# Feed-forward in: two groups of weight columns taken product by product on both sides of the change of token halves

## The chip, the cores and the metric

The kernel runs on one core of one Trainium2 chip. The metric is the device time of one execution in microseconds (us). Of the core's engines, PE (TensorE) multiplies matrices, PEld is its weight load, DVE (VectorE) and ACT (ScalarE) do elementwise work, POOL (GpSimd) does elementwise work too, and SP (SyncE) issues the DMAs here, all from one queue in program order. Every engine works through its own instructions strictly in order.

## The reference, cut to what matters

One layer of a decoder with 2048 tokens and a width of 1024. The attention and gated-linear-attention part ahead of the change is untouched; what the change touches is the first product of the feed-forward block, `nm @ w_ff1`, and what is done with its result:

```python
def rmsnorm(x, g):
    y = x * lax.rsqrt(jnp.mean(x * x, axis=-1, keepdims=True) + EPS)
    return y * g
...
    h = h + jnp.einsum('bsm,md->bsd', mixed, w_out[l])
    nm = rmsnorm(h, mlp_norm_g[l])
    a = jnp.square(jax.nn.relu(jnp.einsum('bsd,df->bsf', nm, w_ff1[l])))   # (2048,1024) x (1024,4096)
    h = h + jnp.einsum('bsf,fd->bsd', a, w_ff2[l])
return rmsnorm(h, final_norm_g)
```

## The kernel before, in words

Every float32 product is made of three products of split numbers: each operand is cut into a high part (a copy in the reduced type, made by ACT) and a low part (operand minus high part, made by DVE), and `mm3` (lines 131 to 134) multiplies high by high, low by high and high by low.

The feed-forward product is done with a scheme of Strassen's kind: seven block products, numbered j = 1 to 7 and taken in the order 1, 2, 5, 6, 3, 4, 7, in place of eight. A *group* g is 256 columns of `w_ff1` against one half (1024) of the tokens. There are NP = 16 groups for each half, so groups 0 to 15 use the first token half and 16 to 31 the second: 32 groups of 7 products, 224 in all, listed in `jobs1`. One product is four calls of `mm3`, 12 matmuls of 128x128 by 128x512, into one PSUM bank. The stationary operand is a weight block (`w1comb`, four buffers in turn), the moving operand a token block `TF[j]` (the tiles `hb...`: for each j a high and a low tile of 2048 columns, 14 tiles that stay in SBUF for a whole token half).

Products 6 and 7 go on adding into the bank in which product 1 stands (`U1`), and product 3 into that of product 5 (`W1B`); so the copy of the bank that is taken after product 1, 5 or 6 has to be done before the later product of the same group starts.

The order of the work is written by hand: inside `tc.manual_schedule(...)` the instructions of all five engines stand as the loop issues them. For each place `at` in `jobs1` the loop calls `slot1(at)`, then steps of the sums over finished groups, then `product1(at)`. `slot1(at)` issues:

- `hi1(at + 3)` on ACT and `lo1(at + 2)` on DVE: the high and low part of the weight block of a coming product (lines 1442 and 1447);
- `evict1(at - 1)`: what is taken out of the bank of the product before: a copy by ACT for j = 1, 6, 5, 4 (lines 1490 to 1494), additions by DVE for j = 2, 3 (one each) and 7 (two; lines 1496 to 1501). The copy of j = 1 and 6 goes to a tile `X`, which is `xt`;
- `squares1(at)`: Relu and Square on ACT (lines 1508, 1509), in pairs, four pairs a group;
- `sum1`, four a group on DVE (line 1454): sums of the raw weight blocks, made in place in `w1raw`, on which some of the coming `hi1` wait;
- `load_w1`, a 1 MB load of the raw weight columns of group g + 2.

When a pair of groups (14 products) is done, `token_sums` makes 28 sums of 128x256 tiles of it (line 1547) during the 14 products that follow, and stores them to `actD` in DRAM, each store eight steps behind its sum in SP's queue. The table `SUMS` gives 11 of them to POOL and 17 to DVE; where `all_pool[0]` is set, POOL makes all 28. The tiles (`acc1`, and the second halves of `xt` and of `gM`) are overwritten by the evictions of the next pair but one.

The change of halves lies at product 112 of 224, the first of group 16. The 14 tiles of `TF` have to be refilled with the second half: for each j a load of 1 MB from `hTD` into a raw tile `rb`, and then, in two parts of 1024 columns each, a high part by ACT (line 549) and a low part by DVE (line 550); 14 such parts in all. In the kernel before, group 15 is the last to use the old tiles and group 16 the first to use the new ones, so a tile `TF[j]` is read by product j of group 15 and again, refilled, seven products later by product j of group 16. The 14 parts are issued at products 106 to 116 (`parts_at`), and three `rb` tiles take the loads in turn.

Of the kernel before, what the change touches and what calls it, by code (L numbers as in the profile page):

```python
# [106 lines left out]
def emit(tc, a, stop=99):  # L107
    nc = tc.nc
    V, A, G, T, SP = nc.vector, nc.scalar, nc.gpsimd, nc.tensor, nc.sync
# [39 lines left out]
    xt = const.tile([128, 1024], F32, name="xt")  # L149
# [61 lines left out]
    hTD = dram.tile([2, 7, 128, 4, 512], F32, name="hTD")  # L211
# [14 lines left out]
    order = (1, 2, 6, 5, 7, 4, 3)  # L226
# [11 lines left out]
    TF = {j: [slot(f"tb{j}", FR) for _ in range(2)] for j in order[:3]}  # L238
# [7 lines left out]
    CX, last, c11, c22, c12, c21 = [t[:, GP * q:GP * q + GP] for t in acc for q in range(2)]  # L246
# [62 lines left out]
    def bank():  # L309
        btags.append(btags.pop(0))  # L310
        return ps(btags[-1])
# [147 lines left out]
    for g in range(NG):  # L459
# [3 lines left out]
        for x, j in enumerate(order):  # L463
            at, b = 7 * g + x, B + L * x
            h, l = (b - 5, b - 3) if L == 2 or (early and x == 0) else (b - 7, b - 4)
            if L == 4 and x == 2:
                h, l = b - 6, b - 3
            if g in (7, 8) or g == 9 and x < 2:
                h, l = b - 3, b - 2
# [51 lines left out]
    rb, oh = bp[:33, :8], view(bp[:33, 8:], (3, 384))  # L521
# [26 lines left out]
    def split(hi, lo, src):  # L548
        A.activation(hi, src, AF.Copy)
        V.tensor_tensor(lo, src, hi.bitcast(F32), op=OP.subtract)  # L550
# [81 lines left out]
    for n in range(7):  # L632
        t = base[7] + 6 + 23 * n // 4
# [99 lines left out]
    with tc.manual_schedule(engines={X.engine for X in (T, V, A, G, SP)}):  # L733
# [78 lines left out]
        for t in range(3, 8):  # L812
            n = t + 1
# [23 lines left out]
        for t in range(12, base[NG] + 10):  # L837
# [436 lines left out]
    for pr in range(4):  # L1274
# [3 lines left out]
        for hh, br in seq:  # L1278
            b = Branch()
            b.h, b.br = 2 * pr + hh, br  # L1280
            m = 4 if br == 2 else 2
            first = len(units)
# [3 lines left out]
            if br == 2 and first:  # L1286
# [61 lines left out]
    gM, gF = gs[:, :D], gs[:, D:2 * D]  # L1348
# [3 lines left out]
    rb, TF, TB = [slot("rb")], {}, {}  # L1352
# [19 lines left out]
    turns = [0]  # L1372
    order = (1, 2, 5, 6, 3, 4, 7)

    def reload(j, half, t=None):

        if t is None:
            t = rb[turns[0] % len(rb)]
            turns[0] += 1
        SP.dma_start(t[:, :2048], hTD[half, j - 1].rearrange("p c s -> p (c s)"))  # L1380

        def rest():
            if j not in TF:
# [29 lines left out]

    w1 = a["w_ff1"].rearrange("o (c p) n -> p (o c) n", p=128)
    NP = FF // 256
    jobs1 = [(g, j) for g in range(2 * NP) for j in order]
    raw1, combs1, acc1 = [], [], []

    def load_w1(g):
        if g < 2 * NP:  # L1420
            if len(raw1) < 2:
                raw1.append(view(slot("w1raw"), (CH, 256)))
            g0 = g % NP * 256
            SP.dma_start(raw1[g % 2], w1[:, :, g0:g0 + 256])

    def blocks1(g):
        r = raw1[g % 2]
        return [r[:, 4 * k:4 * k + 4, n * 128:n * 128 + 128] for n in range(2) for k in range(2)]

    def comb1(at):  # L1430
# [8 lines left out]
    def hi1(at):  # L1439
        if at < len(jobs1):  # L1440
            c, v = comb1(at)
            A.activation(c[:, 0], v, AF.Copy)  # L1442

    def lo1(at):
        if at < len(jobs1):
            c, v = comb1(at)
            V.tensor_tensor(c[:, 1], v, c[:, 0].bitcast(F32), op=OP.subtract)  # L1447

    def sum1(g, n):

        if g < 2 * NP:
            a11, a12, a21, a22 = blocks1(g)
            to, x, y = ((a21, a21, a22), (a11, a21, a11), (a12, a12, a11), (a21, a22, a11))[n]
            V.tensor_tensor(to, x, y, op=OP.subtract if n else OP.add)
# [25 lines left out]
    def blocks_of(g):  # L1480
        return [acc1[g % 4][:, 512 * n:512 * n + 512] for n in range(4)]

    def evict1(at):

        if not 0 <= at < len(jobs1):
            return
        g, j = jobs1[at]
        X, (c11, c12, c21, c22) = xt[:, :512], blocks_of(g)
        if j in (1, 6):
            A.activation(X, U1[g % 2], AF.Copy)  # L1490
        elif j == 5:
            A.activation(c22, W1B[g % 2], AF.Copy)
        elif j == 4:
            A.activation(c21, Y1[g % 2], AF.Copy)
        elif j == 2:
            V.tensor_tensor(c11, Y1[g % 2], X, op=OP.add)
        elif j == 3:
            V.tensor_tensor(c12, W1B[g % 2], X, op=OP.add)
        else:
            V.tensor_tensor(c21, U1[g % 2], c21, op=OP.add)  # L1500
            V.tensor_tensor(c22, U1[g % 2], c22, op=OP.add)
# [8 lines left out]

    def slot1(at):

        g, i = divmod(at, 7)
        hi1(at + 3)
        lo1(at + 2)
        evict1(at - 1)
        squares1(at)
        for k, gg, n in ((5, g + 1, 0), (6, g + 1, 1), (0, g, 2), (1, g, 3)):
            if i == k:
                sum1(gg, n)  # L1520
        if i == 5:
            load_w1(g + 2)

    def act_tiles(g):

# [4 lines left out]
    all_pool = [False]  # L1530
# [219 lines left out]
    for q, at in enumerate(first_of):  # L1750
# [5 lines left out]
        for u in range(4):  # L1756
            n = at + ((-11, -8, -4, -2) if q else (-10, -8, -5, -2))[u]
# [21 lines left out]
            product1(at)  # L1779

    with tc.manual_schedule(engines={X.engine for X in (T, V, A, G, SP)}):
        first, parts_at = 7 * (NP - 1), {}
        for n in range(14):
            parts_at.setdefault(first + 1 + n * 4 // 5, []).append(n // 2)
        halves, begun, half_done = {}, {}, set()
        ts = iter(())
        for at in range(7, len(jobs1)):
            if at == first - 3:
                rb.append(slot("rb"))
                turns[0] = 0  # L1790
                halves.update({n: reload(order[n], 1) for n in range(3)})
            slot1(at)
            all_pool[0] = first < at < first + 13 or at >= len(jobs1) - 6
            if at % 14 == 0:
                for _ in ts:
                    pass
                if at:
                    ts = token_sums(at // 7 - 1)
            for _ in range(SUMS_AT.get(at % 14, 0) if at > 13 else 0):
                next(ts)  # L1800
            product1(at)
            for n in [n for n in begun if n < 4 and begun[n] < at and n + 3 not in halves]:
                halves[n + 3] = reload(order[n + 3], 1)
            for n in parts_at.get(at, ()):
                next(halves[n])
                if n in half_done:
                    begun[n] = at
                half_done.add(n)
            for n in range(2):
                step(2 * (at - len(jobs1)) + n)  # L1810

        for _ in ts:
            pass
        ts = token_sums(2 * NP - 1)
        P, left = {}, None
        for ph in range(2 * NR):
            if PRODUCTS[ph // 2][1]:
                P[ph % 2] = [bank() for _ in range(2)]
            p = P[ph % 2]
            for k in range(8):  # L1820
# [74 lines left out]
```

## Time and profile before

| | |
|---|---|
| median of 3 runs | 2257.23 us (2255.97 to 2259.64) |
| the profiled execution, its own time | 2256.31 us |
| its span, first to last instruction | 2254.5 us |
| mean granted TensorE clock | 0.998 |
| PE busy | 2229.1 us, 99% of the span |
| PEld, DVE, ACT, POOL busy | 85%, 71%, 52%, 36% of the span |

Times inside the trace are us from the start of the span. The first feed-forward product runs from 1057 to 1675 us. A row of the timeline gives the start of an instruction, its length, its engine, its line, operation and tiles, how many it merges, and in brackets the idle time of the engine just before it with what ended it. A row of the waits gives who waited for whom, the total in us, how many times, and the longest. Neighbouring instructions overlap a little, so what one costs its engine is the distance from its start to the next one's start.

### The profile page before, as it was taken

How to read it: one execution, taken by the hardware profiler on the slowest of the kernel's cores; microseconds unless marked ns; L12 is line 12 of the kernel's file. 1: busy time of each engine (PE TensorE's matmuls, PEld its weight loads, DVE VectorE, ACT ScalarE, POOL GpSimd, SP SyncE). 2: the span in 40 equal slices, each digit the busy share in tenths (PEclk: the TensorE clock that was granted, in tenths of full speed). 3: DMA queues.
4: the chain of work that ended last, by engine and by line, in shares of the span. 5: the costliest groups of instructions: out<-in, count | busy, mean ns of one | idle time of the engine just before them, and what ended most of it. 6: DMA issues, size and time to landing. Idle time of an engine off the chain costs nothing.

```text
span 2254.5 us, 34335 instructions
## 1 busy us (share of the span) xinstructions
PE 2229.1 (99%) x12324; PEld 1925.5 (85%) x12324; DVE 1605.4 (71%) x2757; ACT 1164.0 (52%) x2088; POOL 812.5 (36%) x802
## 2 busy tenths in 40 slices
PE   9999999999999999999999999999999999999998
PEld 7978998899999998888888887888888888888886
DVE  6866767746766784446677779777776878758897
ACT  6554446435777782234555557555563333323544
POOL 2111000005378766300122235232345645232665
PEclk9999999999999999999999999999999999999999
DMA  7256444757657864777344457444488653454563
GB/s 207 87 179 194 131 137 153 256 177 238 217 194 240 280 208 150 225 243 263 115 150 145 150 187 226 143 146 148 137 273 306 202 169 130 142 168 149 174 219 112
DMA packets 308267, 415.23 MB, mean 184 GB/s; under 512 B 19509, under 2 KB 236126, under 8 KB 302464
## 3 DMA queue, kind: packets, MB, share of 16 engines
q1 hardware_dynamic: 307950, 412.77, 57.1%
q8 instruction: 97, 1.59, 0.3%
q14 instruction: 74, 0.61, 0.1%
q10 hardware_dynamic: 146, 0.27, 0.0%
HBM read 268.48 MB, written 149.20 MB: 185 GB/s over the span
## 4 chain that ended last, share of the span: by engine, by line
PE 91%; DVE 4%; issue 2%; DMA 1%; ACT 1%; POOL 0%; SPq 0%; POOLq 0%; ACTq 0%; DVEq 0%
PE ps_a L132 11%; PE ps_a L133 11%; PE ps_a L134 11%; PE ps_c L132 9%; PE ps_c L134 8%; PE ps_c L133 8%; PE ps_a L1005 5%; PE ps_d L133 4%; PE ps_d L132 4%; PE ps_d L134 4%; PE ps_d L986 3%; PE ps_c L966 2%; PE ps_c L964 2%; PE ps_o L132 2%; PE ps_o L134 2%; PE ps_o L133 2%
## 5 line engine op out<-in xcount | busy, mean ns | idle before, releaser
L1442 ACT ACTIVATE w1comb<-w1raw 128x512 fp32r<-128x512 f32 x224 | 141.4, 633 | 243.3 <-PE ps_a L134 81.8
L1624 ACT ACTIVATE cs<-rs 128x1024 fp32r<-128x1024 f32 x104 | 109.7, 1055 | 218.7 <-PE ps_c L134 127.8
L1447 DVE TENSOR_TENSOR w1comb<-w1raw,w1comb 128x512 fp32r<-128x512 f32 x224 | 175.8, 786 | 27.5 <-ACT w1comb L1442 27.5
L977 ACT ACTIVATE pe<-pe,O 128x256 f32<-128x256 f32 (+1 forms) x384 | 156.2, 454 | 62.2 <-DVE O L976 57.6
L1005 PE MATMUL ps_a<-v,pt 128*128 128x65 f32 x1200 | 179.0, 252 | 0.0
L1005 PEld LDWEIGHTS ps_a<-v,pt 128*128 128x128 f32 x1200 | 173.4, 193 | 0.9
L986 PE MATMUL ps_d<-ident,pe 128*128 128x128 f32 x600 | 158.1, 278 | 0.0
L976 DVE CUSTOM_DVE_ANT_0 pe<-ps_c,nb 128x256 f32<-128x256 f32 (+1 forms) x384 | 126.7, 361 | 41.5 <-PE ps_d L986 16.8
L132 PE MATMUL ps_a<-hb,w1comb 128*128 128x512 f32 x384 | 149.7, 390 | 0.0
L133 PE MATMUL ps_a<-hb,w1comb 128*128 128x512 f32 x384 | 149.5, 389 | 0.0
L134 PE MATMUL ps_a<-hb,w1comb 128*128 128x512 f32 x384 | 149.4, 389 | 0.0
L1666 DVE TENSOR_TENSOR ct<-rt,ct 128x1024 fp32r<-128x1024 f32 x68 | 129.8, 1909 | 18.8 <-ACT ct L1662 18.8
L133 PE MATMUL ps_c<-ct,cs 128*128 128x512 f32 x360 | 140.1, 389 | 0.0
L132 PE MATMUL ps_c<-ct,cs 128*128 128x512 f32 x360 | 140.1, 389 | 0.0
L134 PE MATMUL ps_c<-ct,cs 128*128 128x512 f32 x360 | 140.1, 389 | 0.0
L163 POOL TENSOR_TENSOR stats<-stats,mhalf 128x1 f32<-128x1 f32 (+1 forms) x64 | 50.0, 783 | 242.6 <-DVE stats L162 242.5
L918 POOL CAST qp<-qs 128x512 fp32r<-128x512 f32 x64 | 66.6, 1126 | 180.2 <-DMA srD<-xp 164.1
L1547 POOL TENSOR_TENSOR acc<-acc 128x256 f32<-128x256 f32 x75 | 69.1, 931 | 160.9 <-DVE acc L1547 148.6
L1631 DVE SCALAR_TENSOR_TENSOR cs<-rs,cs 128x1024 fp32r<-128x1024 f32 (+1 forms) x56 | 100.0, 1793 | 29.6 <-ACT cs L1624 29.3
L293 ACT ACTIVATE wcomb<-wraw 128x512 fp32r<-128x512 f32 (+2 forms) x119 | 89.1, 756 | 60.2 <-DVE wraw L305 25.2
L1547 POOL TENSOR_TENSOR xt<-acc,acc 128x256 f32<-128x256 f32 x32 | 28.1, 878 | 226.7 <-ACT acc L1509 210.3
L986 PEld LDWEIGHTS ps_d<-ident,pe 128*128 128x128 f32 x600 | 108.0, 185 | 0.3
(434 smaller groups left out, 7319.4 us busy)
## 6 DMA issues: line engine op xcount, KB each, us to landing
rs<-actD SPq DMA_DIRECT2D x103, 512.0 KB, 3.7
actD<-acc SPq DMA_DIRECT2D x288, 128.0 KB, 2.9
w1raw<-w_ff SPq DMA_DIRECT2D x32, 1024.0 KB, 6.5
rt<-w_ff SPq DMA_DIRECT2D x24, 1024.0 KB, 7.2
k<-kD SPq DMA_DIRECT2D x16, 1024.0 KB, 8.5
rb<-hTD SPq DMA_DIRECT2D x13, 1024.0 KB, 7.6
wraw<-w_in SPq DMA_DIRECT2D x12, 1024.0 KB, 5.3
cmb<-boD SPq DMA_DIRECT2D x16, 528.0 KB, 6.2
```

The costliest lines, as they stand in the source:

```text
L132: T.matmul(out, sh, mh, start=first, stop=False, skip_group_check=more)
L133: T.matmul(out, sl, mh, start=False, stop=False, skip_group_check=more)
L134: T.matmul(out, sh, ml, start=False, stop=last, skip_group_check=more)
L976: V.tensor_tensor_reduce(p, s, bias, scale=1.0, scalar=BIG, op0=OP.add, op1=OP.min, accum_out=nm)
L977: A.activation(p, p, AF.Exp, bias=nm, scale=-1.0)
L986: T.transpose(pb[:, i * 128:i * 128 + 128], src, ident)
L1005: T.matmul(self.b.opsum[:, n % 4], self.pt[:, i * 128:i * 128 + 128], self.b.v[:, blk, cols], start=first, stop=last)
L1442: A.activation(c[:, 0], v, AF.Copy)
L1447: V.tensor_tensor(c[:, 1], v, c[:, 0].bitcast(F32), op=OP.subtract)
L1624: A.activation(v[:, 0], x, AF.Copy, scale=float(PRODUCTS[ph // 2][2]))
L1631: V.scalar_tensor_tensor(v[:, 1], x, -1.0, v[:, 0].bitcast(F32), op0=OP.mult, op1=OP.subtract)
L1666: V.tensor_tensor(v[:, 1], x, v[:, 0].bitcast(F32), op=OP.subtract)
```

## The change

Four things are altered together.

1. `jobs1`, the order of the products. Groups 14 and 15 (the last two of the first half) and groups 16 and 17 (the first two of the second) are taken product by product: j = 1 of group 14, j = 1 of 15, j = 2 of 14, j = 2 of 15 and so on. All other groups stand as they did. A tile `TF[j]` is now read last by one of two neighbouring products and is needed again, refilled, from 12 products after them.
2. The refill: the 14 parts are spread over products 100 to 122 (`first` is 98), one part in a place, the high part at place `at` and the low part at the head of place `at + 1`. Their loads are 512 KB each, into the two halves of one `rb` tile, and the load of part m + 2 is issued behind the low part of m.
3. The weight sums stand one place earlier (in all groups), and there are four `w1raw` buffers in place of two. `X` is `xt` for even groups and `gM` for odd ones.
4. `all_pool` is set for places 100 to 124, where it was 106 to 117.

```diff
-    jobs1 = [(g, j) for g in range(2 * NP) for j in order]
+    jobs1 = []
+    for g in range(0, 2 * NP, 2):
+        if g in (NP - 2, NP):
+            jobs1.extend((g + k, j) for j in order for k in range(2))
+        else:
+            jobs1.extend((g + k, j) for k in range(2) for j in order)
+    at_of = {job: at for at, job in enumerate(jobs1)}
+    sums_at, loads_at = {}, {}
+    for g in range(2 * NP):
+        for n, j, dt in ((0, 5, 5), (1, 6, 5), (2, 3, 5), (3, 7, 6)):
+            if g or n > 1:
+                sums_at.setdefault(max(0, at_of[g, j] - dt), []).append((g, n))
+        loads_at[at_of[g, 1] - 9] = g
...
-            SP.dma_start(raw1[g % 2], w1[:, :, g0:g0 + 256])
+            SP.dma_start(raw1[g % 4], w1[:, :, g0:g0 + 256])
...
-        X, (c11, c12, c21, c22) = xt[:, :512], blocks_of(g)
+        X, (c11, c12, c21, c22) = (xt, gM)[g % 2][:, :512], blocks_of(g)
...
-        for k, gg, n in ((5, g + 1, 0), (6, g + 1, 1), (0, g, 2), (1, g, 3)):
-            if i == k:
-                sum1(gg, n)
-        if i == 5:
-            load_w1(g + 2)
+        for g, n in sums_at.get(at, ()):
+            sum1(g, n)
+        if at in loads_at:
+            load_w1(loads_at[at])
...
-        first, parts_at = 7 * (NP - 1), {}
-        for n in range(14):
-            parts_at.setdefault(first + 1 + n * 4 // 5, []).append(n // 2)
+        first = 7 * (NP - 2)
+        parts_at = {first + 2 + m * 22 // 13: m for m in range(14)}
+        change = []
+
+        def load_part(m):
+            if not change:
+                t = slot("rb")
+                change.extend(t[:, 1024 * h:1024 * h + 1024] for h in range(2))
+            if m < 14:
+                v = hTD[1, order[m // 2] - 1].rearrange("p c s -> p (c s)")
+                SP.dma_start(change[m % 2], v[:, m % 2 * 1024:m % 2 * 1024 + 1024])
...
+            m = parts_at.get(at - 1)
+            if m is not None:
+                h, l = part_of(m)
+                V.tensor_tensor(l, change[m % 2], h.bitcast(F32), op=OP.subtract)
             slot1(at)
-            all_pool[0] = first < at < first + 13 or at >= len(jobs1) - 6
+            all_pool[0] = first + 1 < at < first + 27 or at >= len(jobs1) - 6
...
             product1(at)
-            for n in [n for n in begun if n < 4 and begun[n] < at and n + 3 not in halves]:
-                halves[n + 3] = reload(order[n + 3], 1)
-            for n in parts_at.get(at, ()):
-                next(halves[n])
...
+            if m is not None:
+                load_part(m + 2)
+            if at in parts_at:
+                m = parts_at[at]
+                A.activation(part_of(m)[0], change[m % 2], AF.Copy)
```

Three places show what moves. First ACT, at products 113 to 115 before. `hb...<-rb` is a high token part, `w1comb<-w1raw` the high part of a weight block, `acc<-ps` or `xt<-ps` the copy out of a bank, and 1508 and 1509 a pair of Relu and Square.

```order
L1442 ACTIVATE w1comb<-w1raw 128x512
L1490 ACTIVATE xt<-ps_a 128x512
L1508 ACTIVATE acc_10730<-acc_10730 128x512
L1509 ACTIVATE acc_10730<-acc_10730 128x512
L549 ACTIVATE hb_10744<-rb 128x1024
L1442 ACTIVATE w1comb<-w1raw 128x512
L1508 ACTIVATE acc_10730<-acc_10730 128x512
L1509 ACTIVATE acc_10730<-acc_10730 128x512
L549 ACTIVATE hb_10795<-rb 128x1024 x2
L1442 ACTIVATE w1comb<-w1raw 128x512
L1492 ACTIVATE acc_10727<-ps_d 128x512
```

The same engine now, at products 113 to 115, where two pairs of Relu and Square fall together:

```order
L1520 ACTIVATE acc_10731<-acc_10731 128x512
L1521 ACTIVATE acc_10731<-acc_10731 128x512
L1520 ACTIVATE acc_10730<-acc_10730 128x512
L1521 ACTIVATE acc_10730<-acc_10730 128x512
L1830 ACTIVATE hb_10745<-rb 128x1024
L1454 ACTIVATE w1comb<-w1raw 128x512
L1502 ACTIVATE gs<-ps_c 128x512
L1520 ACTIVATE acc_10731<-acc_10731 128x512
L1521 ACTIVATE acc_10731<-acc_10731 128x512
L1454 ACTIVATE w1comb<-w1raw 128x512
L1830 ACTIVATE hb_10745<-rb 128x1024
```

Ahead of the copy of product 5's bank (`L1492`) there stood two high token parts with nothing between them; now there is never more than one between two weight parts, and the copies of the banks stand further from the products that need them.

Second DVE, before, at products 114 to 116; `hb...<-rb,hb` is a low token part, `w1comb<-w1raw,w1comb` the low part of a weight block, `w1raw<-w1raw` a weight sum:

```order
L1447 TENSOR_TENSOR w1comb<-w1raw,w1comb 128x512
L1496 TENSOR_TENSOR acc_10727<-ps_c,xt 128x512
L550 TENSOR_TENSOR hb_10796<-rb,hb_10795 128x1024 x2
L1447 TENSOR_TENSOR w1comb<-w1raw,w1comb 128x512
L550 TENSOR_TENSOR hb_10818<-rb,hb_10817 128x1024
L1447 TENSOR_TENSOR w1comb<-w1raw,w1comb 128x512
L550 TENSOR_TENSOR hb_10818<-rb,hb_10817 128x1024
```

and now, at products 115 to 117:

```order
L1508 TENSOR_TENSOR acc_10728<-ps_d,xt 128x512
L1466 TENSOR_TENSOR w1raw<-w1raw 128x4x128
L1815 TENSOR_TENSOR hb_10746<-rb,hb_10745 128x1024
L1459 TENSOR_TENSOR w1comb<-w1raw,w1comb 128x512
L1508 TENSOR_TENSOR acc_10729<-ps_c,gs 128x512
L1466 TENSOR_TENSOR w1raw<-w1raw 128x4x128
L1815 TENSOR_TENSOR hb_10796<-rb,hb_10795 128x1024
```

The low token parts went from four in three products to at most one in a product; each stands ahead of a weight part.

Third SP's queue, behind the sums of groups 12 and 13. Before, the loads into `rb` (1 MB each) stood in it so (products 109 to 111):

```order
L1537 DMA actD_105<-acc1_10728 128x256
L1380 DMA rb_10711<-hTD_104 128x2048
L1424 DMA w1raw_10716<-w_ff1 128x8x256
L1537 DMA actD_105<-xt_77 128x256
L1537 DMA actD_105<-gs_9147 128x256
L1537 DMA actD_105<-acc1_10728 128x256
L1380 DMA rb_12897<-hTD_104 128x2048
```

and now, at products 111 to 115, the loads of parts 9 and 10 (the row of `rb` with x2) stand behind the last stores of those sums:

```order
L1802 DMA rb_12789<-hTD_104 128x1024
L1547 DMA actD_105<-gs_9147 128x256
L1547 DMA actD_105<-acc1_10728 128x256 x2
L1547 DMA actD_105<-acc1_10729 128x256
L1547 DMA actD_105<-acc1_10728 128x256 x2
L1547 DMA actD_105<-acc1_10729 128x256
L1802 DMA rb_12789<-hTD_104 128x1024 x2
L1547 DMA actD_105<-acc1_10731 128x256 x2
```

The 1 MB loads that stood between the stores are now 512 KB loads, and parts 9 and 10 are behind all the stores of the sums of groups 12 and 13.

More of the change, by code (lines that the diff above doesn't have):

```diff
@@ L1420, in load_w1 @@
         if g < 2 * NP:
-            if len(raw1) < 2:
+            if len(raw1) < 4:
                 raw1.append(view(slot("w1raw"), (CH, 256)))
             g0 = g % NP * 256
-            SP.dma_start(raw1[g % 2], w1[:, :, g0:g0 + 256])
+            SP.dma_start(raw1[g % 4], w1[:, :, g0:g0 + 256])
     def blocks1(g):
-        r = raw1[g % 2]
+        r = raw1[g % 4]
         return [r[:, 4 * k:4 * k + 4, n * 128:n * 128 + 128] for n in range(2) for k in range(2)]
@@ L1511, in slot1 @@
     def slot1(at):
-        g, i = divmod(at, 7)
         hi1(at + 3)
@@ L1781, in emit, with part_of @@
     with tc.manual_schedule(engines={X.engine for X in (T, V, A, G, SP)}):
-        first, parts_at = 7 * (NP - 1), {}
-        for n in range(14):
-            parts_at.setdefault(first + 1 + n * 4 // 5, []).append(n // 2)
-        halves, begun, half_done = {}, {}, set()
+        first = 7 * (NP - 2)
[8 more added lines that the diff above has]
+                SP.dma_start(change[m % 2], v[:, m % 2 * 1024:m % 2 * 1024 + 1024])
+        def part_of(m):
+            return [v[:, m % 2 * 1024:m % 2 * 1024 + 1024] for v in TF[order[m // 2]]]
         ts = iter(())
         for at in range(7, len(jobs1)):
[L1788 to L1791, printed above, removed]
+            if at == first - 1:
+                load_part(0)
+                load_part(1)
+            m = parts_at.get(at - 1)
+            if m is not None:
+                h, l = part_of(m)
+                V.tensor_tensor(l, change[m % 2], h.bitcast(F32), op=OP.subtract)
             slot1(at)
-            all_pool[0] = first < at < first + 13 or at >= len(jobs1) - 6
+            all_pool[0] = first + 1 < at < first + 27 or at >= len(jobs1) - 6
             if at % 14 == 0:
@@ L1801, in emit @@
             product1(at)
-            for n in [n for n in begun if n < 4 and begun[n] < at and n + 3 not in halves]:
-                halves[n + 3] = reload(order[n + 3], 1)
-            for n in parts_at.get(at, ()):
-                next(halves[n])
-                if n in half_done:
-                    begun[n] = at
-                half_done.add(n)
+            if m is not None:
[3 more added lines that the diff above has]
+                A.activation(part_of(m)[0], change[m % 2], AF.Copy)
             for n in range(2):
```

## The prediction

> **What bounds the kernel now.** First the page: its span, busy times and chain of waits.
>
> ```profile
> span 2254.5 us, 34335 instructions
> PE 2229.1 (99%) x12324; PEld 1925.5 (85%) x12324; DVE 1605.4 (71%) x2757; ACT 1164.0 (52%) x2088; POOL 812.5 (36%) x802
> PE 91%; DVE 4%; issue 2%; DMA 1%; ACT 1%; POOL 0%; SPq 0%; POOLq 0%; ACTq 0%; DVEq 0%
> ```
>
> The chain is PE's. As the change removes no matmul, all that it can win is time in which PE stood still or ran slowly near the change of halves. So I read PE's waits next, then PE's timeline around product 112.
>
> ```profile
> PE ps_d L132 <- ACT acc L1492: 3.4, 1, 3.4
> PE ps_c L133 <- DVE w1comb L1447: 1.0, 1, 1.0
> ```
> ```profile
> 1325.15 0.39 PE L132 MATMUL ps_a<-hb,w1comb 128*128 128x512 f32 x1
> ...
> 1327.87 0.39 PE L132 MATMUL ps_c<-hb,w1comb 128*128 128x512 f32 x1
> ...
> 1367.49 0.50 PE L133 MATMUL ps_c<-hb,w1comb 128*128 128x512 f32 x1 [1.04 <-DVE w1comb L1447]
> ...
> 1379.57 0.50 PE L132 MATMUL ps_d<-hb,w1comb 128*128 128x512 f32 x1 [3.41 <-ACT acc L1492]
> ...
> 1384.02 0.40 PE L132 MATMUL ps_c<-hb,w1comb 128*128 128x512 f32 x1
> ...
> 1408.53 0.39 PE L132 MATMUL ps_a<-hb,w1comb 128*128 128x512 f32 x1
> ```
>
> The rows at 1325.15 and 1327.87 are the starts of products 98 and 99: a product that waits for nothing takes 2.72 us. Product 126 starts at 1408.53. The 28 products 98 to 125 took 83.38 us, where 28 x 2.72 = 76.16: **7.22 us are lost there**, and that is all there is to win. Both of PE's waits on the product's own inputs in this stage are in it: 1.04 at product 113, and 3.41 at 116 (j = 3 of group 16, which adds into the bank that line 1492 had still to copy). After the second, product 116 itself is slow; the windows show why:
>
> ```profile
> 1348.00:1365.00 17.00, 17.00 (x76) 13.84 (x76) 14.67 (x14) 13.83 (x21) 14.58 (x12) 1.00 0.61 171
> 1376.00:1379.57 3.57, 0.16 (x2) 0.00 (x1) 3.35 (x5) 3.57 (x6) 2.79 (x3) 1.00 0.93 335
> 1379.57:1384.00 4.43, 4.43 (x12) 3.50 (x13) 4.43 (x4) 3.99 (x6) 4.27 (x4) 0.61 0.14 48
> ```
>
> The columns are the stretch, its length, busy PE, PEld, DVE, ACT, POOL, then PE's granted clock. After 3.4 us of idleness the clock was 0.61 and product 116 took 1384.02 - 1379.57 = 4.45 us, 1.73 too many; this goes with the wait. In the first and third stretch DVE, ACT and POOL are at 80 to 100%: around the change the helpers are full, not PE.
>
> **The prices.** ACT ahead of the long wait:
>
> ```profile
> 1374.83 0.61 ACT L1442 ACTIVATE w1comb<-w1raw 128x512 fp32r<-128x512 f32 x1
> 1375.35 0.61 ACT L1508 ACTIVATE acc<-acc 128x512 f32<-128x512 f32 x1
> 1375.99 0.63 ACT L1509 ACTIVATE acc<-acc 128x512 f32<-128x512 f32 x1
> 1376.53 1.99 ACT L549 ACTIVATE hb<-rb 128x1024 fp32r<-128x1024 f32 x2
> 1378.42 0.61 ACT L1442 ACTIVATE w1comb<-w1raw 128x512 fp32r<-128x512 f32 x1
> 1378.94 0.58 ACT L1492 ACTIVATE acc<-ps_d 128x512 f32<-128x512 f32 x1
> 1379.42 0.62 ACT L1508 ACTIVATE acc<-acc 128x512 f32<-128x512 f32 x1
> ```
>
> From start to start: a weight part 0.52, a Relu and Square pair 1.18, a high token part 0.95, a copy out of a bank 0.48. Two token parts (1.89) stood straight ahead of L1492. DVE:
>
> ```profile
> 1364.49 2.35 DVE L550 TENSOR_TENSOR hb<-rb,hb 128x1024 fp32r<-128x1024 f32 x2
> 1366.76 0.68 DVE L1447 TENSOR_TENSOR w1comb<-w1raw,w1comb 128x512 fp32r<-128x512 f32 x1
> 1367.36 0.68 DVE L1454 TENSOR_TENSOR w1raw<-w1raw 128x512 f32<-128x512 f32 x1
> ...
> 1380.79 1.22 DVE L1447 TENSOR_TENSOR w1comb<-w1raw,w1comb 128x512 fp32r<-128x512 f32 x1
> 1381.93 1.75 DVE L550 TENSOR_TENSOR hb<-rb,hb 128x1024 fp32r<-128x1024 f32 x1
> 1383.60 1.22 DVE L1447 TENSOR_TENSOR w1comb<-w1raw,w1comb 128x512 fp32r<-128x512 f32 x1
> ```
>
> While POOL rests, a 128x512 operation costs 0.60 and a low token part 1.14 (2.27 for two). While POOL works (1376.7 to 1388, below), the same cost 1.14 and 1.67: 0.54 more each. POOL's sums (line 1547) in the two bursts in which they are all POOL's:
>
> ```profile
> 1332.69 0.95 POOL L1547 TENSOR_TENSOR xt<-acc,acc 128x256 f32<-128x256 f32 x1 [11.46 <-ACT acc L1509]
> ...
> 1346.65 0.89 POOL L1547 TENSOR_TENSOR xt<-acc,acc 128x256 f32<-128x256 f32 x1 [0.99 <-DMA actD<-xt]
> ...
> 1349.36 0.74 POOL L1547 TENSOR_TENSOR gs<-acc,acc 128x256 f32<-128x256 f32 x1
> ...
> 1361.10 1.72 POOL L1547 TENSOR_TENSOR acc<-acc,acc 128x256 f32<-128x256 f32 x1
> 1376.70 0.73 POOL L1547 TENSOR_TENSOR xt<-acc,acc 128x256 f32<-128x256 f32 x1 [13.88 <-ACT acc L1509]
> ...
> 1387.06 1.19 POOL L1547 TENSOR_TENSOR acc<-acc,acc 128x256 f32<-128x256 f32 x1
> ```
>
> 13 sums from 1346.65 to 1362.82 and 9 from 1376.70 to 1388.25: 27.72 us for 22, **1.26 us a sum**, between 0.74 free and 1.72 at worst. What they cost DVE is read from the groups of 1346 to 1389:
>
> ```profile
> L550 DVE TENSOR_TENSOR hb<-rb,hb 128x1024 fp32r<-128x1024 f32 x14 | 20.7, 1493 | 3.6 <-ACT hb L549 3.6
> L1447 DVE TENSOR_TENSOR w1comb<-w1raw,w1comb 128x512 fp32r<-128x512 f32 x13 | 12.6, 973 | 0.0
> L1454 DVE TENSOR_TENSOR w1raw<-w1raw 128x512 f32<-128x512 f32 x7 | 5.3, 757 | 0.0
> ```
>
> Against free lengths of 1.21 (1.14 and 0.07 of overlap) and 0.68 that is 3.8 + 3.8 + 0.5 = 8.1 us more, over 22 sums: **0.37 us of DVE for each sum of POOL's**, between 0 and 0.54.
>
> The Trainium skill, in "SBUF — State Buffer" (section Who interferes with whom), says that a DVE operation with two SBUF inputs and a POOL operation that reads SBUF exclude each other, the loser waiting the other out in full. By that rule a sum could cost DVE up to 0.74, and 56 sums 41 us; the rows bear out half of it.
>
> **The change part by part.** Places are counted from product 98: place s is product 98 + s.
>
> *Order of the products.* PE runs the same 224 x 12 matmuls: 0. A copy out of the bank of j = 5 now has three products until j = 3 needs it, where it had one; j = 1 to 6 and 6 to 7 have five. The 3.41 us wait, with its 1.73 of slow clock, loses its cause unless ACT falls two products behind.
>
> *ACT.* Its fullest place is s = 15: weight part 0.52, copy 0.48, two pairs 2.36, token part 0.95 = 4.31 us, against 2.72. Places 14 and 16 have 1.70 and 2.18, so it is 1.6 behind at most, and catches up in two places. Hidden: weight parts are issued three products ahead. Cost 0. All 28 places: 28 x 0.52 + 16 x 0.48 + 16 x 1.18 + 14 x 0.95 = 54 us of 76.
>
> *DVE.* 28 weight parts, 16 sums, 16 additions out of banks at 0.60 and 14 token parts at 1.14: 52 us, and 56 x 0.37 = 21 for POOL's sums: 73 of 76 us. So not the total but the bunching decides. Work in the tight places, with 0.8 for POOL's sums (2.72 / 1.26 = 2.2 a place, x 0.37): s = 13 and 14, a token part and four others, 3.54 + 0.8 = 4.34 each; 15: 2.0; 16: 2.7; 17: 2.6; 18: 3.74; 19: 2.5; 20: 2.0; 21: 3.1; 22: 1.4. Behind 2.72 a place DVE is late by 1.6, 3.2, 2.5, 2.5, 2.4, 3.4, 3.2, 2.5, 2.9, 1.6 us. The weight part of product s + 2 has to be done within 5.44 us of the start of s, behind its place's token part: at 18, 2.4 + 1.14 + 0.60 and up to 1.1 = 5.2; at 19, 3.4 + 1.74 and 0.5 to 1.1 = 5.6 to 6.2. Product 119 (s = 21) is late by 0.2 to 0.8 us. With 0.54 a sum in place of 0.37, the same table gives 2 us over products 118 and 119; with 0.2, nothing. **I take 0.5 us**, bounds 0 and 2.
>
> *POOL and SP.* All 56 sums of the two pairs go to POOL. The first may start when the squares of the pair before are done, at 1332.69, that is 7.54 us or 2.8 places behind product 98. 28 x 1.26 = 35.3 us is 13 places: done at s = 15.8. Parts 9 and 10 are loaded behind the last store of these sums. Part 9 is wanted by ACT at 17.2, its low part stands ahead of the weight part of product 118 (s = 20). The load:
>
> ```profile
> rs<-actD SPq DMA_DIRECT2D x103, 512.0 KB, 3.7
> ...
> rb<-hTD SPq DMA_DIRECT2D x13, 1024.0 KB, 7.6
> ```
>
> At 512 KB, 3.7 us or 1.4 places (half of the 7.6 for a whole `rb` agrees): landed at 17.2, just in time. ACT 0.95, DVE's token part and weight part 1.14 + 0.60 and up to 1.1 make 1.4 places more: ready at 18.6 of 20. Cost 0 with 1.4 places in hand; no gain, as no wait of before is on it. The second pair's sums run from 16.8 to 29.8, and the first eviction into their tiles is at 30. Cost 0, bound 1 us.
>
> *Sums one place earlier, four raw buffers.* Same instructions, nothing added. They lengthen the time between a sum and the ACT copy that waits for it from one place to two:
>
> ```profile
> ACT w1comb L1442 <- DVE w1raw L1454: 8.9, 4, 4.1
> ```
>
> These 8.9 us of ACT between 1346 and 1389 shrink; they were not on PE's path except through ACT's lateness. A load is issued nine places ahead as before. Elsewhere in the stage PE waits for nothing, so this gives 0 there.
>
> Sum against the profiled execution's 2256.31: - 7.22 + 0.5 + 0.1 (rows at 0.24 for 0.23 when a buffer is just in time) = 2249.7. That execution lay 0.92 below the median of 2257.23, so the median forecast is **2250.6 us**.
>
> **The rivals.** *Half of the gain.* DVE is late oftener: collisions at 0.54, and ACT in turn late on squares and sums that wait for DVE. 2 us from the table, and as much again if product 119's wait falls on ACT's fullest stretch: 2.5 to 5 us lost, 2252.5 to 2255. For it: 73 of 76 us. Against it: DVE's peaks are single, and collisions cease while it waits.
>
> *POOL's sums late (slower than before).* At 1.6 a sum (POOL's rows at their worst) 28 take 16.5 places and end at 19.3. Part 9 lands at 20.7, ACT is done at 21.0, DVE at 22.0 (1.67 + 1.14 us): product 118 starts 2.0 places late, 5.5 us, with the slow clock of above 1.73 more. The second pair ends at 35.8, PE being 2.7 places later; the eviction at 30 waits 1.2 places for a store, of which some 1 us reaches PE. With the 0.5 from above 8.7 us in place of 7.22: 2258.7 in the median. It decides from 1.4 us a sum on (end at 17.2, all 1.4 places used up). Against it: 1.26 was measured with DVE at 86% and over.
>
> *The wait moves.* Earlier sums block DVE on a weight load in the ordinary groups, or the next stage waits for what it was hidden behind: 2257, no change. Loads are issued nine places (24 us) ahead, and nothing at the end of the stage depends on absolute time.
>
> **How the numbers follow.** The forecast, less than 2.5 us lost: 0.64. Half of the gain: 0.22. POOL late: 0.10. The wait moves: 0.04. This kernel's runs can tell about 0.2%, 4.5 us, from no change: the line is at 2252.7. Faster: 0.64 and a sixth of the next, less a little for the forecast's own upper end, 0.66. Slower than 2261.7 needs POOL's case with more than 10 us, 0.04. Same: 0.30. The range begins at nothing lost from the fastest run shown (2255.97 - 7.2 = 2248.8) and goes to the end of the second case, 2255.5, leaving out POOL's case and the moved wait.
>
> **What would show it.** Right: products 98 to 126 take 76 to 78.5 us; no PE wait on L1504 (the copy of j = 5) and no clock below 0.9 there; DVE's token parts mostly at 1.2 to 1.8; POOL's sums of groups 12 and 13 end near 1368, and part 9's load is issued then. Wrong: a PE wait at products 118 or 119 over 2 us, ACT idle on the DMA of `rb`, or POOL's sums over 1.4 us each. The weakest step is the 1.26 and 0.37, taken from 22 sums and used for 56.

## The result and the profile after

| | before | after |
|---|---|---|
| median, same chips | 2257.24 us (2253.22 to 2260.67, 21 runs) | 2253.36 us (2248.62 to 2255.84, 21 runs) |
| ratio after to before | | 0.9981, 95% interval 0.9975 to 0.9987 |
| the profiled execution, its own time | 2256.31 us | 2253.79 us |
| products 98 to 125, 76.16 us if nothing is lost | 83.38 us | 79.21 us |

The kernel is faster by 0.19%, 3.9 us by the medians; the forecast was 6.6 us. This is the page of the kernel after, its span and busy times:

```profile
span 2252.0 us, 34353 instructions
PE 2229.8 (99%) x12324; PEld 1927.1 (86%) x12324; DVE 1620.1 (72%) x2739; ACT 1164.5 (52%) x2088; POOL 846.5 (38%) x820
```

There are as many matmuls as before, and POOL is busy 34 us longer. Next come PE's waits and the timeline rows at which it waits, with the first matmul of product 98 (1326.87) and of product 126 (1406.08):

```profile
PE ps_c L133 <- DVE w1comb L1459: 1.3, 2, 1.0
PE ps_o L133 <- DVE w1comb L1459: 0.5, 1, 0.5
```
```profile
1326.87 0.39 PE L132 MATMUL ps_a<-hb,w1comb 128*128 128x512 f32 x1
...
1354.78 0.50 PE L133 MATMUL ps_c<-hb,w1comb 128*128 128x512 f32 x1 [0.32 <-DVE w1comb L1459]
...
1358.30 0.50 PE L133 MATMUL ps_o<-hb,w1comb 128*128 128x512 f32 x1 [0.51 <-DVE w1comb L1459]
...
1387.09 0.50 PE L133 MATMUL ps_c<-hb,w1comb 128*128 128x512 f32 x1 [0.99 <-DVE w1comb L1459]
...
1406.08 0.39 PE L132 MATMUL ps_a<-hb,w1comb 128*128 128x512 f32 x1
```

1406.08 - 1326.87 = 79.21: 3.05 us are still lost, where 7.22 were. The wait for the copy of j = 5, with its slow clock, is gone. What is lost sits in two places: products 108, 109 and 111 are 0.62, 0.82 and 0.10 us longer than 2.72 (1.54 together), products 118 and 119 0.18 and 1.33 (1.51). Every wait that the trace shows there is for the low part of a weight block on DVE; each makes its product some 0.3 us longer than the bracket says (0.32 and 0.62, 0.51 and 0.82, 0.99 and 1.33). The stage as a whole started 1.73 us later in this execution (1059.20 against 1057.47); its start scatters, from 1055.18 to 1061.53 over the runs below, with 1061.00 in the other execution of this kernel. So the profiled times differ by 2.52, and the 28 products by 4.17, which is nearer to the medians' 3.9.

The windows (stretch, length, busy PE, PEld, DVE, ACT, POOL, clock, DMA share, GB/s): the 28 products, and the two places:

```profile
1326.87:1406.08 79.21, 77.39 (x337) 62.72 (x336) 69.48 (x72) 54.22 (x86) 60.24 (x52) 1.00 0.68 206
1346.00:1360.00 14.00, 13.17 (x57) 10.28 (x56) 13.11 (x12) 6.73 (x11) 13.41 (x12) 1.00 0.90 292
1380.00:1390.00 10.00, 9.01 (x40) 6.86 (x39) 10.00 (x10) 7.33 (x13) 9.77 (x9) 1.00 0.85 255
```

DVE and POOL are nearly full in both places (13.11 and 13.41 of 14 us, 10.00 and 9.77 of 10). In the first, DMA is at 0.90 besides and ACT is half idle. These are the rows behind the first place, from SP's queue, ACT and DVE:

```profile
1341.84 0.43 SPq L1436 DMA_DIRECT2D w1raw<-w_ff  x1
1342.94 0.88 SPq L1436 DMA_DIRECT2D w1raw<-w_ff  x1
1347.39 0.38 SPq L1802 DMA_DIRECT2D rb<-hTD  x1
```
```profile
1354.52 1.06 ACT L1830 ACTIVATE hb<-rb 128x1024 fp32r<-128x1024 f32 x1 [4.57 <-DMA rb<-hTD]
```
```profile
1351.82 1.75 DVE L1815 TENSOR_TENSOR hb<-rb,hb 128x1024 fp32r<-128x1024 f32 x1
1353.50 1.22 DVE L1459 TENSOR_TENSOR w1comb<-w1raw,w1comb 128x512 fp32r<-128x512 f32 x1
1355.62 1.49 DVE L1815 TENSOR_TENSOR hb<-rb,hb 128x1024 fp32r<-128x1024 f32 x1 [0.89 <-ACT hb L1830]
1357.03 1.22 DVE L1459 TENSOR_TENSOR w1comb<-w1raw,w1comb 128x512 fp32r<-128x512 f32 x1
```

Read backwards: product 109 waited at 1358.30 for a weight part of 1.22 us which stood behind the low part of token part 4 (1355.62), which waited for ACT's high part (1354.52), which waited 4.57 us for its load. That load was issued at 1347.39, behind two 1 MB weight loads, and took 7.1 us. Product 108 likewise waited for the weight part at 1353.50 behind low part 3. At the second place the same pair stands without any wait, only slowed by POOL:

```profile
1384.14 1.76 DVE L1815 TENSOR_TENSOR hb<-rb,hb 128x1024 fp32r<-128x1024 f32 x1
1385.83 2.36 DVE L1459 TENSOR_TENSOR w1comb<-w1raw,w1comb 128x512 fp32r<-128x512 f32 x2
```

From this come three candidates for what is still lost: the late load, the bunching of DVE's work with POOL's collisions, and the place of the low token part in DVE's queue, ahead of the weight part. There is also a question on the gain: which of the four edits made it.

### The profile page after: what moved, and what is told of

It reads as the page before. It is cut to its first block, busy times and chain, and to the rows that moved or that the text cites. A ratio compares the mean times of both kernels' runs of the same rounds, so it can differ in the third digit from the quotient of the medians.

```text
span 2252.0 us, 34353 instructions
## 1 busy us (share of the span) xinstructions
PE 2229.8 (99%) x12324; PEld 1927.1 (86%) x12324; DVE 1620.1 (72%) x2739; ACT 1164.5 (52%) x2088; POOL 846.5 (38%) x820
## 5 line engine op out<-in xcount | busy, mean ns | idle before, releaser
L1459 DVE TENSOR_TENSOR w1comb<-w1raw,w1comb 128x512 fp32r<-128x512 f32 x224 | 188.2, 843 | 25.3 <-ACT w1comb L1454 25.2
L132 PE MATMUL ps_a<-hb,w1comb 128*128 128x512 f32 x376 | 146.5, 390 | 0.0
L133 PE MATMUL ps_a<-hb,w1comb 128*128 128x512 f32 x376 | 146.5, 390 | 0.0
L134 PE MATMUL ps_a<-hb,w1comb 128*128 128x512 f32 x376 | 146.3, 389 | 0.0
L1557 POOL TENSOR_TENSOR acc<-acc 128x256 f32<-128x256 f32 x83 | 83.7, 1020 | 138.7 <-DVE acc L1557 126.5
```

Source lines behind the costliest of these rows:

```text
L132: T.matmul(out, sh, mh, start=first, stop=False, skip_group_check=more)
L133: T.matmul(out, sl, mh, start=False, stop=False, skip_group_check=more)
L134: T.matmul(out, sh, ml, start=False, stop=last, skip_group_check=more)
L1557: (G if pool or all_pool[0] else V).tensor_tensor(t[l], t[x], t[y], op=OP.add if op == "+" else OP.subtract)
```

## The experiments

"Lost" is the time from the start of product 98 to that of product 126, less 76.16, in the profiled execution of each run. The ratios of the medians are to the kernel before, run beside it, with 95% intervals. Each expectation below was written ahead of its run; "theory" and "rival" are the two outcomes that it tells apart.

| | lost, us | ratio |
|---|---|---|
| before | 7.22 | 1 |
| after | 3.05 | 0.9981 (0.9975 to 0.9987) |
| after, run again beside the last two | 3.02 | 0.9983 (0.9974 to 0.9992) |
| earlier weight loads | 2.37 | 0.9982 (0.9972 to 0.9992) |
| flatter places | 2.91 | 0.9982 (0.9973 to 0.9992) |
| both | 2.19 | 0.9970 (0.9958 to 0.9982) |
| new order and parts, old weight sums | 6.48 | 1.0008 (0.9998 to 1.0018) |
| old order and parts, earlier weight sums | 5.80 | 1.0001 (0.9990 to 1.0013) |
| token sums shared with DVE | 3.90 | 0.9993 (0.9983 to 1.0003) |
| no token sums | 0.00 | 0.9973 (0.9963 to 0.9982) |
| both, weight parts first on DVE | 0.01 | 0.9968 (0.9959 to 0.9977) |
| after, weight parts first on DVE | 0.00 | 0.9969 (0.9958 to 0.9979) |
| the same with old weight sums | 2.37 | 0.9982 (0.9973 to 0.9990) |

**The late load.** The weight loads of groups 16 and 17 are issued before the first token parts.

```diff
-        loads_at[at_of[g, 1] - 9] = g
+        loads_at[{NP: 93, NP + 1: 96}.get(g, at_of[g, 1] - 9)] = g
```

> The weight loads of groups 16 and 17 (1 MB each) are issued at places 93 and 96 instead of 103 and 104, ahead of the first token parts. Theory (loads): products 108 and 109 started 0.62 and 0.82 us late because the 512 KB load of token part 4 stood behind these two loads and took 7.1 us. Then both waits vanish, the load of part 4 lands in under 5 us, and products 98 to 125 take 77.8 us (79.2 less 1.4). Rival (DVE and ACT are late by themselves, from the squares and low parts): the waits at 108 and 109 stay within 0.4 us of what they were, and the 28 products take 79 us or more. Both leave the 1.5 us at 118 and 119.

The 28 products took 78.53 us, between the theory's 77.8 and the rival's 79. The load of part 4 now took 4.3 us:

```profile
1345.34 0.32 SPq L1802 DMA_DIRECT2D rb<-hTD  x1
```
```profile
1349.64 1.06 ACT L1830 ACTIVATE hb<-rb 128x1024 fp32r<-128x1024 f32 x1 [1.68 <-DMA rb<-hTD]
```

Product 109's loss shrank from 0.82 to 0.10, product 108's stayed (0.61). So the theory holds for one of the two; the other doesn't go with this load.

**Flatter places.**

```diff
-        parts_at = {first + 2 + m * 22 // 13: m for m in range(14)}
+        parts_at = {first + p: m for m, p in enumerate((2, 4, 5, 7, 8, 10, 11, 14, 15, 17, 18, 20, 21, 23))}
```

> The 14 token parts stand at places 2, 4, 5, 7, 8, 10, 11, 14, 15, 17, 18, 20, 21, 23 of the two pairs, so that no low part shares a place with four other DVE operations. Theory (bunching on DVE): the 1.5 us at products 118 and 119 fall to 0.3 or less, and products 98 to 125 take 77.7 to 78 us if those at 108 and 109 stay, less if part 4's load is issued earlier too. Rival (DVE's total, 73 of 76 us, is what counts, not the bunching): the same 1.5 us are lost, at other products, and the 28 take 79 us or more.

The 28 products took 79.07 us, as the rival had it: the loss at 118 and 119 went down to 1.00 (119) and came back as 0.92 at product 122; product 108 no longer lost anything, 109 still 0.73. So bunching in these places alone is not the cause; whether it is DVE's total, as the rival says, this run can't tell.

**Both.** The two edits together.

> Both edits together, the earlier weight loads and the flatter places. If the two losses are separate and each has its own cause, products 98 to 125 take 76.2 to 76.8 us, 2.4 to 3 us less than in the changed kernel, ratio to the kernel before 0.9968 to 0.9972. Rival (the helpers are full, and a loss taken away in one place comes back in another): 78 us or more, ratio 0.9976 or above.

The 28 products took 78.35 us, which is the rival's case (78 or more): the loss came back in another place. The ratio 0.9970 is of five runs, and its interval holds both outcomes. Nothing is lost at 108 and 109; 1.02 at product 119 and 0.90 at 122 remain. These are PE's waits, and DVE ahead of product 119:

```profile
PE ps_c L133 <- DVE w1comb L1459: 1.3, 2, 0.7
```
```profile
1378.35 1.76 DVE L1815 TENSOR_TENSOR hb<-rb,hb 128x1024 fp32r<-128x1024 f32 x1
1380.04 2.37 DVE L1459 TENSOR_TENSOR w1comb<-w1raw,w1comb 128x512 fp32r<-128x512 f32 x2
```

Again a weight part stands behind a token part.

**The order of products without the earlier sums.**

```diff
-        for n, j, dt in ((0, 5, 5), (1, 6, 5), (2, 3, 5), (3, 7, 6)):
+        for n, j, dt in ((0, 5, 4), (1, 6, 4), (2, 3, 4), (3, 7, 5)):
```

> The new order of products, parts and loads, but the weight sums at their old distance (4, 4, 4, 5 products ahead in place of 5, 5, 5, 6). Theory (the order of products carries the gain): no wait on the copy of j = 5, the 28 products take 79 to 80.5 us, ratio to the kernel before within 0.0005 of the changed kernel's 0.9981. Rival (the earlier sums are needed, since ACT waited 8.9 us for them before): ACT waits for weight sums 5 us or more, this reaches PE, and the 28 products take 81 us or more, ratio 0.999 or above.

The theory fell: the 28 products took 82.64 us, and 1.1 us more were lost behind them (products 129 and 130). These are ACT's longest wait in total from 1327 to 1409, which is about the 28 products, and the group of low token parts on DVE (its idle time and what ended it stand behind the bar):

```profile
ACT w1comb L1454 <- DVE w1raw L1466: 14.0, 9, 2.6
```
```profile
L1815 DVE TENSOR_TENSOR hb<-rb,hb 128x1024 fp32r<-128x1024 f32 x14 | 21.5, 1538 | 12.1 <-ACT hb L1830 12.1
```

With a sum one place ahead of its copy, ACT waited 14.0 us for DVE's sums, and DVE 12.1 for ACT's high parts that stood behind those copies: the two engines held each other up. In the changed kernel the two waits are 0.6 and 9.2.

**The earlier sums without the order.** The kernel before, with

```diff
-        for k, gg, n in ((5, g + 1, 0), (6, g + 1, 1), (0, g, 2), (1, g, 3)):
+        for k, gg, n in ((4, g + 1, 0), (5, g + 1, 1), (6, g + 1, 2), (0, g, 3)):
+            if at == 0 and n == 3:
+                sum1(0, 2)
```

> The kernel before, in its old order of products and token parts, with nothing changed but the weight sums, one product earlier (two raw buffers as before). With the order and parts alone (the run before this one) nothing was won; this is the other half. Theory A (order and earlier sums only win together: one removes the copy that stood before product 116, the other the waits of ACT on weight sums): PE still waits 2.5 us or more for the copy of j = 5, products 98 to 125 take 82 to 84 us, ratio to the kernel before 0.9992 to 1.0004. Theory B (the earlier sums are the whole gain): 79 to 80.5 us, ratio 0.998 to 0.9988.

The 28 products took 81.96 us, just under theory A's 82 to 84, and the ratio didn't change, as A had it. PE's wait for the copy of j = 5 is smaller than A's 2.5 us, but it is there, with its cause, two token parts ahead of the copy on ACT:

```profile
PE ps_d L132 <- ACT acc L1492: 1.1, 1, 1.1
```
```profile
1376.95 1.99 ACT L549 ACTIVATE hb<-rb 128x1024 fp32r<-128x1024 f32 x2
1378.84 0.61 ACT L1442 ACTIVATE w1comb<-w1raw 128x512 fp32r<-128x512 f32 x1
1379.36 0.57 ACT L1492 ACTIVATE acc<-ps_d 128x512 f32<-128x512 f32 x1
```

Neither half alone gives a gain that the runs show; together they give 0.19%. The other half holds the order of the products, the refill, the four raw buffers and the range of `all_pool`; what each of these does by itself was not run.

**Token sums shared.**

```diff
-            all_pool[0] = first + 1 < at < first + 27 or at >= len(jobs1) - 6
+            all_pool[0] = at >= len(jobs1) - 6
```

> The changed kernel, but DVE and POOL share the token sums of the two pairs as they do elsewhere (11 of 28 on POOL, 17 on DVE) in place of all 28 on POOL. Theory (DVE is full, and an addition of its own of about 0.5 us costs it more than the 0.37 us that a POOL sum takes from it): DVE has 52 + 34 x 0.5 + 22 x 0.37 = 77 us of work for 76, and products 98 to 125 take 80 us or more, ratio 0.9985 or above. Rival (collisions with POOL are dearer than 0.37): fewer POOL sums make them 78.5 us or less, ratio 0.9978 or below.

The 28 products took 80.06 us, on the theory's line. DVE is slowed less by POOL (a weight part takes 0.84 us on average in place of 1.08), but its own sums use that up: it is busy 70.23 us, where it was 69.48 in the changed kernel. So giving POOL all the sums in these places is worth 0.85 us of the profile against sharing them. The old range of `all_pool`, places 106 to 117, was not run with the new order.

**No token sums.**

```diff
+            no_sums[0] = first + 1 < at < first + 27
...
-                (G if pool or all_pool[0] else V).tensor_tensor(...)
+                if not no_sums[0]:
+                    (G if pool or all_pool[0] else V).tensor_tensor(...)
```

> The changed kernel without the token sums of the two pairs (POOL does nothing there; the stores stay): left out is that part of the computation. It measures all that POOL's sums cost. Theory (DVE's lengthened operations are the cause of the 3 us that are still lost): weight parts and low parts fall to 0.68 and 1.21 us, the waits at 118 and 119 vanish, and products 98 to 125 take 76.2 to 77.7 us; of the loss at 108 and 109 what belongs to the loads alone stays (0 to 1.4 us). Rival (the ring of two half tiles, load, ACT, DVE, load again, is the limit): ACT still waits 5 us or more for loads of token parts, and the 28 products take 78.5 us or more.

The 28 products took 76.16 us, nothing lost. These are the window of the 28 products, the load of part 4 (issued, used), and the weight parts:

```profile
1326.84:1403.00 76.16, 76.16 (x337) 63.06 (x336) 54.94 (x76) 54.08 (x86) 1.44 (x2) 1.00 0.75 228
```
```profile
1345.81 0.37 SPq L1803 DMA_DIRECT2D rb<-hTD  x1
```
```profile
1353.07 1.06 ACT L1832 ACTIVATE hb<-rb 128x1024 fp32r<-128x1024 f32 x1 [3.15 <-DMA rb<-hTD]
```
```profile
L1459 DVE TENSOR_TENSOR w1comb<-w1raw,w1comb 128x512 fp32r<-128x512 f32 x30 | 20.3, 683 | 1.1 <-ACT w1comb L1454 1.1
```

The load took 7.3 us here too, and ACT waited for loads 5.9 us in all: alone, the late load costs nothing. DVE was busy 54.94 us for 76 operations, where it was 69.48 for 72 with POOL at work. Four operations of 0.60 us are 2.4, so by this estimate POOL's 52 sums took some 17 us of DVE's time (69.48 - 52.5). The Trainium skill, in "SBUF — State Buffer" (section Who interferes with whom), calls the ports that the two share an exclusive lock. The trace agrees in that both engines are slower side by side: POOL was busy 60.24 us with its 52 sums, which would be 38.5 us at the 0.74 of a sum beside a resting DVE. That the ports are what does it, no run here shows.

**Weight parts first, on top of both.**

```diff
-    def slot1(at):
+    def slot1(at, low=lambda: None):
         hi1(at + 3)
         lo1(at + 2)
+        low()
...
-                V.tensor_tensor(l, change[m % 2], h.bitcast(F32), op=OP.subtract)
-            slot1(at)
+                slot1(at, lambda: V.tensor_tensor(l, change[m % 2], h.bitcast(F32), op=OP.subtract))
+            else:
+                slot1(at)
```

> The version with earlier weight loads and flatter places (2.2 us still lost, at products 119 and 122, each time on a weight part that stood behind a low token part on DVE), with one edit more: in each place DVE does the weight part first and the low token part behind it. Theory (DVE's order): no weight part waits for a token part of its own place; products 119 and 122 lose 0.3 us or less together, the 28 products take 76.3 to 77 us, 1.3 to 2 us less, ratio to the kernel before 0.9962 to 0.9966. Rival (the ring of two half tiles is full, and a later low part makes the next load later): the loss moves to other products and the 28 take 78 us or more, ratio 0.997 or above.

The 28 products took 76.17 us, nothing lost, as the theory had it. The ratio 0.9968 lies between the theory's 0.9962 to 0.9966 and the rival's 0.997, and its interval holds both, so here the profile decides.

**Weight parts first, alone.** The changed kernel with only the edit above.

> The changed kernel with one edit alone: in each place DVE does the weight part first and the low token part behind it (weight loads and places as in the change). Theory (each microsecond still lost is a weight part that stood behind a low token part in DVE's queue): the late load of part 4 stays, ACT waits 4 us or more for it, but it reaches no weight part of the same place; products 98 to 125 take 76.2 to 77 us, ratio to the kernel before 0.9966 to 0.9971. Rival (earlier loads and flatter places are needed too, since DVE still waits for ACT one place later): 77.5 us or more, ratio 0.9973 or above.

The 28 products took 76.16 us. These are their window, the high part of part 4 on ACT, and DVE at the place that was shown of the changed kernel:

```profile
1327.50:1403.66 76.16, 76.16 (x337) 63.08 (x336) 68.20 (x72) 53.66 (x86) 59.08 (x49) 1.00 0.70 206
```
```profile
1355.16 1.06 ACT L1832 ACTIVATE hb<-rb 128x1024 fp32r<-128x1024 f32 x1 [4.58 <-DMA rb<-hTD]
```
```profile
1350.62 1.22 DVE L1459 TENSOR_TENSOR w1comb<-w1raw,w1comb 128x512 fp32r<-128x512 f32 x1
1351.76 1.75 DVE L1816 TENSOR_TENSOR hb<-rb,hb 128x1024 fp32r<-128x1024 f32 x1
1353.44 1.22 DVE L1459 TENSOR_TENSOR w1comb<-w1raw,w1comb 128x512 fp32r<-128x512 f32 x1
1356.25 1.49 DVE L1816 TENSOR_TENSOR hb<-rb,hb 128x1024 fp32r<-128x1024 f32 x1 [1.59 <-ACT hb L1832]
```

DVE does the same 72 operations in nearly the same time (68.20 us, where it was 69.48), the weight parts take the same 1.22 here, ACT still waits 4.58 us for the load. But the weight part of product 109 (1353.44) is now ahead of the low part that waits (1356.25), and all of the 3 us is back. So the queue order turned lateness on DVE into a loss on PE; the load and POOL set how late the weight part came. Without POOL's sums the same order cost nothing, so the loss needed both.

**The same with the old distance of the sums.**

> The same edit, but the weight sums at their old distance (4, 4, 4, 5 products ahead). With the old distance and the low parts first, 6.5 us were lost in the 28 products. Theory A (those came from the same queue order, low parts ahead of sums and weight parts): 78 us or less. Theory B (a sum one place ahead of its copy on ACT binds the two engines place by place, whatever the order within a place): ACT waits 8 us or more on weight sums, and the 28 products take 79 us or more.

The 28 products took 78.53 us, between A's 78 and B's 79. ACT's waits on sums were B's:

```profile
ACT w1comb L1454 <- DVE w1raw L1466: 8.4, 6, 2.2
```

With weight parts first the earlier sums are worth 2.4 us, with token parts first 3.4 (6.48 - 3.05) in these products. Their cost has a part of its own and a part that the queue order adds.

**The changed kernel again.**

> The changed kernel as it is, on the same chip as the two others, to compare with: ratio to the kernel before 0.9975 to 0.9987, products 98 to 125 79.2 us, if the waits at 108, 109, 118 and 119 are not an accident of one execution.

The 28 products took 79.18 us, with losses at the same products 108, 109, 118 and 119 of the same size within 0.05 us: they belong to the program.

## Why the prediction was right, and where not

*The wait for j = 5.* Right: there is no wait on L1504, no clock under 1.00 in the windows, and nothing like the 4.45 us that product 116 took. But the prediction named the order of the products as the cause. The runs show that order and parts alone give nothing that shows, since other waits of nearly as much take its place (6.48 us lost of 7.22).

*Sums one place earlier, priced at 0.* This is the step that failed. The 8.9 us that ACT waited for sums between 1346 and 1389 (10.3 from 1327 to 1409) were read and set aside as "not on PE's path except through ACT's lateness". That exception was the case: in the new order with the old distance, ACT's waits on sums came to 14.0 us from 1327 to 1409, and 3.4 us more of PE were lost than with the earlier sums. For the order alone the same working would have been some 6 us off (6.48 lost where it gives 0.6). That the sum came out in spite of it is luck: the change makes both edits.

*DVE late at product 119, 0.5 us with bounds 0 and 2.* The place and the sign were right, the size was 1.5. The table put the late weight part there because it counted the token part ahead of it, and it used nearly the right prices: 0.33 us of DVE for a POOL sum (17 us over 52 sums, by the estimate above; forecast 0.37) and weight parts of up to 1.22. What it did not do is ask whether that token part had to stand there.

*Loads at a cost of 0, "0.1" for rows.* What was lost ahead of product 112 was missed by 1.4: products 108, 109 and 111 lost 1.54. The 3.7 us of a 512 KB load were taken for all parts, and the timing was worked out for part 9 alone. Part 4's load met two 1 MB loads and took 7.1. Half of the 1.54 goes with it: with those two issued earlier, 109 lost 0.72 less. The 0.6 of product 108 stayed then and left with the flatter places; the table has no late DVE there, since it begins with s = 13. One of the prediction's own signs of being wrong came true, ACT idle on the loads of `rb`:

```profile
ACT hb L1830 <- DMA rb<-hTD: 7.8, 5, 4.6
```

*POOL.* The price of a sum was right. The 28 sums of groups 12 and 13, first and last row:

```profile
1334.89 0.74 POOL L1557 TENSOR_TENSOR xt<-acc,acc 128x256 f32<-128x256 f32 x1 [11.94 <-ACT acc L1521]
...
1367.19 1.19 POOL L1557 TENSOR_TENSOR acc<-acc,acc 128x256 f32<-128x256 f32 x1
```

(1368.38 - 1334.89) / 28 = 1.20 us a sum, forecast 1.26; they end at 1368.38, forecast "near 1368". The rival of late sums, from 1.4 us a sum on, didn't occur. Part 9's load did not follow at once, though: SP issued it at 1371.28, as it also stands behind low part 7, which DVE began at 1369.50. PE lost nothing by that.

*The sum.* Forecast 0.6 us lost of 7.22, measured 3.05. The difference of 2.4 is 1.0 at 118 and 119 and 1.4 at 108 to 111. The median came 2.8 above the forecast; it lies inside the range because the range was drawn to the end of the second case. What occurred is that case, the rival "half of the gain" with its chance of 0.22, by its number (2.5 to 5 us lost), and in part by its mechanism: DVE was late beside POOL's sums, but the second part came at products 108 to 111, half of it with a load, and not from ACT's fullest stretch. The products took 79.21 us, where 76 to 78.5 was the sign of being right. The gain of 0.19% is just under the 0.2% that the prediction took as the least that can be told from no change; with 21 runs the interval is clear of 1.

## What to carry to other kernels

Where one engine's queue carries both work with a near deadline and work that only has to be done some time, the near one goes first in each place: here one moved line was worth 3 us of 7, with no work removed and little change in what POOL takes of DVE. Before a wait is put down as off the path, work out where it stands once the wait in front of it is gone; two waits that cover for each other show nothing when one of them is taken away. A transfer's time taken from one place doesn't hold at another: look at what is queued and in flight when it is issued.

The changed kernel with weight parts first is the best version that the experiments gave with little edited, 0.9969 (0.9958 to 0.9979) of the time before; earlier loads and flatter places on top of it add nothing that shows (0.9968).

## What was not expected of the hardware

A 512 KB load took 7.1 us from its issue to ACT's use of it behind two 1 MB loads (7.3 in the run without token sums), 4.3 with those two issued earlier; the median of the 103 loads from which the prediction took its price was 3.7.

POOL's 128x256 sums took 1.20 us each beside a busy DVE and 0.74 beside a resting one, and they took some 17 us of DVE's time. Running both at once was still the cheaper way: with 17 of 28 sums on DVE 0.85 us more was lost.
